# A strided slice by DMA alone: loads into 64 partitions, a new order of batches, and all stores on one queue

## The chip, the cores and the metric

One core of a Trainium2 chip. The metric is the device time of one execution in microseconds, median of several runs; the profile's span is some 1.7 us shorter. Where a run is compared with the kernel before, both ran in turn on the same chip.

## The reference

```python
def setup_inputs():
    batch, seq, dim = 32, 1024, 512
    return {"x": np.random.randn(batch, seq, dim).astype(np.float32), "start": 0, "stop": 512, "stride": 2}

def reference(x, start, stop, stride):
    return x[:, start:stop:stride, :].astype(np.float32)
```

From each of 32 batches 256 rows of 2 KB are kept, every second one of the first 512. 16.78 MB are read and 16.78 MB written. Nothing is computed.

## The kernel before

Half of the kept rows go straight from memory to memory ("direct copies", issued by ACT). The other half go into the partitions ("loads", issued by SP) and from there to the output ("stores"). Of each batch the direct copies take the kept rows of one parity, `apart(b)`, and the loads those of the other.

```python
def apart(b):
    return 1 - (b >> 1 & 1)

def two(t, b, step, parity):          # rows of one parity, of batches b and b+step
    return t[b : b + step + 1 : step].rearrange("b (p two) d -> two p b d", two=2)[parity]
...
    held = io.tile([P, B, D], x.dtype, name="held")          # P = 128
    ...
    for g in groups:                                          # 0, 8, 16, 24
        for i, (b, step) in enumerate(((0, 5), (2, 5), (1, 3), (3, 3))):
            b += g
            at = g + 2 * i
            sp.dma_start(held[:, at : at + 2], two(src, at, 1, 1 - apart(at))).then_inc(loaded[g // EIGHT], 16)
            act.dma_start(two(out, b, step, apart(b)), two(src, b, step, apart(b))).then_inc(done[1], 16)
    for g in groups:
        for queue in (sp, act):
            queue.wait_ge(loaded[g // EIGHT], 16 * 4)
        for b in range(g, g + 4):
            k = b % 2
            to = two(out, b, 4, 1 - apart(b))
            (sp, act)[k].dma_start(to, held[:, b : b + 5 : 4]).then_inc(done[k], 16)
```

Every transfer is 512 KB in packets of 2 KB, one row each.

Of the kernel before, what the change touches and what calls it, by code (L numbers as in the profile page):

```python
# [3 lines left out]

EIGHT = 8


def apart(b):


    return 1 - (b >> 1 & 1)


def two(t, b, step, parity):

    return t[b : b + step + 1 : step].rearrange("b (p two) d -> two p b d", two=2)[parity]


def kernel(tc, x, start, stop, stride, out):




    nc = tc.nc
    src = x[:, start:stop:stride, :]
    B, rows, D = out.shape
    P = rows // 2
    sp, act = nc.sync, nc.scalar
    groups = range(0, B, EIGHT)
    with tc.tile_pool(name="io", bufs=1) as io:  # L30
        held = io.tile([P, B, D], x.dtype, name="held")
        with tc.tile_critical():
            loaded = [nc.alloc_semaphore(name=f"loaded{g}") for g in groups]
            done = [nc.alloc_semaphore(name=f"done{i}") for i in range(2)]
            for g in groups:
                for i, (b, step) in enumerate(((0, 5), (2, 5), (1, 3), (3, 3))):
                    b += g
                    at = g + 2 * i
                    sp.dma_start(held[:, at : at + 2], two(src, at, 1, 1 - apart(at))).then_inc(loaded[g // EIGHT], 16)
                    act.dma_start(two(out, b, step, apart(b)), two(src, b, step, apart(b))).then_inc(done[1], 16)  # L40
            for g in groups:
                for queue in (sp, act):
                    queue.wait_ge(loaded[g // EIGHT], 16 * 4)
                for b in range(g, g + 4):
                    k = b % 2
                    to = two(out, b, 4, 1 - apart(b))
                    (sp, act)[k].dma_start(to, held[:, b : b + 5 : 4]).then_inc(done[k], 16)
            sp.wait_ge(done[0], 16 * (B // 4))
            sp.wait_ge(done[1], 16 * (B // 2 + B // 4))


# [1 line left out]
_INS = ['x', 'start', 'stop', 'stride']  # L53
_OUTS = [((32, 256, 512), 'float32')]

_NUMBERS = {'start': 0, 'stop': 512, 'stride': 2}


def kernel(**inputs):
    import numpy as _np  # L60
    import concourse.bacc as _bacc
    import concourse.tile as _tile
    from concourse import mybir as _mybir
    from concourse.bass_utils import run_bass_kernel_spmd as _run

    nc = _bacc.Bacc("TRN2", target_bir_lowering=False, num_devices=1)  # L66
    arrays, args = {}, []
    for name in _INS:
        if name in _NUMBERS:
            args.append(_NUMBERS[name])  # L70
            continue
        a = _np.ascontiguousarray(inputs[name])
        if a.dtype.kind in "iu":
            a = a.astype(_np.int64)
        arrays[f"in_{name}_dram"] = a
        args.append(nc.dram_tensor(f"in_{name}_dram", a.shape, _mybir.dt.from_np(a.dtype), kind="ExternalInput").ap())
    for i, (shape, dtype) in enumerate(_OUTS):
        dt = _mybir.dt.from_np(_np.dtype(dtype))
        args.append(nc.dram_tensor(f"out_{i}_dram", shape, dt, kind="ExternalOutput").ap())
    with _tile.TileContext(nc) as tc:  # L80
        kernel(tc, *args)
    r = _run(nc, [arrays], core_ids=[0])
    got = tuple(r.results[0][f"out_{i}_dram"] for i in range(len(_OUTS)))
    return got[0]
```

## Time and profile before

| | before |
|---|---|
| time, median (7 runs beside the first experiments) | 81.32 us |
| span of the profiled run | 79.6 us |
| first data packet | 2.0 us |
| read stage: loads and direct copies, to the last one's start | 2.0 to 54.4 us |
| store stage, to the last packet's start | 54.4 to 77.8 us |

There is no compute engine to look at. One reads the GB/s row of the page (40 equal slices of the span), the table of stretches, and the packet records, which give queue, start and duration of every 2 KB packet. The lines themselves are in the prediction below.

### The profile page before, as it was taken

What the parts mean: (1) busy time and instruction counts of PE and PEld (TensorE: products, weight loads), DVE (VectorE), ACT (ScalarE), POOL (GpSimd) and SP (SyncE); (2) the same over time, 40 slices, a digit from 0 to 9 for tenths busy, and PEclk for the clock granted to TensorE, in tenths of its full rate; (3) what the DMA queues carried; (4) which work ended last, traced back from release to release, by engine and by line L of the source; (5) the groups of instructions that cost most, each with busy time, mean ns of one, the idle gap of its engine ahead of it and who ended that gap; (6) DMA issues with size and microseconds to landing.
All of it is one profiled execution on the core that took longest, in us unless ns stands there. A gap on an engine that the chain in (4) does not pass through costs nothing. (4 is left out here: it accounts for less than half of the span.)

```text
span 79.6 us, 99 instructions
## 1 busy us (share of the span) xinstructions
POOL 0.2 (0%) x4
## 2 busy tenths in 40 slices
POOL 0000000000000000000000000000000000000000
DMA  0897999999999999999989999999999999999930
GB/s 0 258 293 231 329 282 360 364 313 322 373 300 363 367 339 369 295 327 311 259 295 398 389 361 332 297 348 407 408 408 364 351 347 348 355 357 356 350 114 5
DMA packets 13056, 25.17 MB, mean 316 GB/s; under 512 B 768, under 2 KB 768, under 8 KB 13056
## 3 DMA queue, kind: packets, MB, share of 16 engines
q1 hardware_dynamic: 6528, 12.58, 48.0%
q10 hardware_dynamic: 6528, 12.58, 47.3%
HBM read 16.78 MB, written 16.78 MB: 422 GB/s over the span
## 5 line engine op out<-in xcount | busy, mean ns | idle before, releaser
L66 POOL MEMSET const-bfloat16-1.0<- 128x1 bf16 x1 | 0.1, 101 | 0.0
L66 POOL MEMSET const-uint8-127<- 128x1 uint8 x1 | 0.1, 101 | 0.0
L66 POOL MEMSET const-float32-0.0<- 128x1 f32 x1 | 0.1, 98 | 0.2 <-issue 0.2
L66 POOL MEMSET const-float32-1.0<- 128x1 f32 x1 | 0.1, 98 | 0.0
## 6 DMA issues: line engine op xcount, KB each, us to landing
out_dram<-in_x_dram ACTq DMA_DIRECT2D x16, 512.0 KB, 22.7
held<-in_x_dram SPq DMA_DIRECT2D x16, 512.0 KB, 22.1
out_dram<-held SPq DMA_DIRECT2D x8, 512.0 KB, 21.5
out_dram<-held ACTq DMA_DIRECT2D x8, 512.0 KB, 21.4
```

The source lines that it names most:

```text
L66: nc = _bacc.Bacc("TRN2", target_bir_lowering=False, num_devices=1)
```

## The change

The stated intent: batches are loaded into 64 partitions each, in an order by which loads and direct copies read different parts of the memory, and the stores go over neighbouring batches on one queue. The diff, cut to its core:

```diff
+def pairs(t, parity):
+    return t.rearrange("(p n two) d -> two p n d", n=2, two=2)[parity]
...
+    order = [g + i for kind in ((0, 3), (1, 2)) for g in groups for i in kind]
+    sets = [order[i : i + 4] for i in range(0, len(order), 4)]
-        held = io.tile([P, B, D], x.dtype, name="held")
+        held = io.tile([P, B // 2, 2, D], x.dtype, name="held")
...
-            for g in groups:                       # loads and direct copies as above
-                ...
-            for g in groups:                       # waits by group, stores on two queues
-                ...
+            for set_of in sets:
+                for b in set_of:
+                    act.dma_start(two(out, b, 4, apart(b)), two(src, b, 4, apart(b))).then_inc(done[1], 16)
+                    for at in (b, b + 4):
+                        first = at % 2 * (P // 2)
+                        to = held[first : first + P // 2, at // 2]
+                        sp.dma_start(to, pairs(src[at], 1 - apart(at))).then_inc(loaded, 16)
+            sp.wait_ge(loaded, 16 * B)
+            for b in range(0, B, 2):
+                to = out[b : b + 2].rearrange("b r d -> (b r) d")
+                sp.dma_start(pairs(to, 1 - apart(b)), held[:, b // 2]).then_inc(done[0], 16)
```

Four things change at once: the loads' form (64 partitions, 256 KB each instead of 512), the order with the pairs of the direct copies (always b with b+4), the form of the stores, and one queue behind one wait for all loads. Below, "kind A" are the batches whose two lowest bits are 00 or 11, taken first; "kind B" those with 01 or 10.

More of the change, by code (lines that the diff above doesn't have):

```diff
@@ L29 @@
     groups = range(0, B, EIGHT)
+    order = [g + i for kind in ((0, 3), (1, 2)) for g in groups for i in kind]
+    sets = [order[i : i + 4] for i in range(0, len(order), 4)]
     with tc.tile_pool(name="io", bufs=1) as io:
-        held = io.tile([P, B, D], x.dtype, name="held")
+        held = io.tile([P, B // 2, 2, D], x.dtype, name="held")
         with tc.tile_critical():
-            loaded = [nc.alloc_semaphore(name=f"loaded{g}") for g in groups]
+            loaded = nc.alloc_semaphore(name="loaded")
             done = [nc.alloc_semaphore(name=f"done{i}") for i in range(2)]
-            for g in groups:
-                for i, (b, step) in enumerate(((0, 5), (2, 5), (1, 3), (3, 3))):
-                    b += g
-                    at = g + 2 * i
-                    sp.dma_start(held[:, at : at + 2], two(src, at, 1, 1 - apart(at))).then_inc(loaded[g // EIGHT], 16)
-                    act.dma_start(two(out, b, step, apart(b)), two(src, b, step, apart(b))).then_inc(done[1], 16)
-            for g in groups:
-                for queue in (sp, act):
-                    queue.wait_ge(loaded[g // EIGHT], 16 * 4)
-                for b in range(g, g + 4):
-                    k = b % 2
-                    to = two(out, b, 4, 1 - apart(b))
-                    (sp, act)[k].dma_start(to, held[:, b : b + 5 : 4]).then_inc(done[k], 16)
-            sp.wait_ge(done[0], 16 * (B // 4))
-            sp.wait_ge(done[1], 16 * (B // 2 + B // 4))
+            for set_of in sets:
[9 more added lines that the diff above has]
+                sp.dma_start(pairs(to, 1 - apart(b)), held[:, b // 2]).then_inc(done[0], 16)
+            sp.wait_ge(done[0], 16 * (B // 2))
+            sp.wait_ge(done[1], 16 * (B // 2))
 _INS = ['x', 'start', 'stop', 'stride']
```

## The prediction

> **What bounds the kernel now.** I read the page first, then the table of stretches, then the DMA view of single stretches. The page shows no compute at all, and the chain of waits is useless here, because it ends at the four constants that are set at the start. What remains is the DMA part.
>
> ```profile
> DMA  0897999999999999999989999999999999999930
> GB/s 0 258 293 231 329 282 360 364 313 322 373 300 363 367 339 369 295 327 311 259 295 398 389 361 332 297 348 407 408 408 364 351 347 348 355 357 356 350 114 5
> q1 hardware_dynamic: 6528, 12.58, 48.0%
> q10 hardware_dynamic: 6528, 12.58, 47.3%
> held<-in_x_dram SPq DMA_DIRECT2D x16, 512.0 KB, 22.1
> out_dram<-held SPq DMA_DIRECT2D x8, 512.0 KB, 21.5
> ```
>
> The digit row says that the 16 DMA engines are busy from end to end; the GB/s row below it says that the same 90% or more carries anything from 231 to 408 GB/s. So the engines have work all the time, and what varies is how long one packet takes. Each queue has 12.58 MB and an equal share. An issue waits some 22 us to land, so each queue has several 512 KB transfers behind the one that runs. The engines' wait list confirms it: SP waited only 0.7 us in all for loads before the stores. No semaphore is on the path today.
>
> Three stages show in the table of stretches (columns: length, POOL, clock, DMA share, GB/s):
>
> ```profile
> 2.00:14.00 12.00, 0.00 (x0) 1.00 0.93 293
> 14.00:52.00 38.00, 0.00 (x0) 1.00 1.03 335
> 52.00:60.00 8.00, 0.00 (x0) 1.00 1.04 395
> 60.00:75.00 15.00, 0.00 (x0) 1.00 1.06 353
> ```
>
> The first data packet starts at 2.0 us. Up to about 53 us the loads and the direct copies run side by side (16.78 MB: 3.51 MB in the first row, 12.75 MB in the second, the last 0.5 MB in 1.3 us of the third). From there to 77.8 us, where the last packet starts, the stores run (8.39 MB in 24.5 us, a mean of 342 GB/s with the ragged end), and 1.8 us later the span ends.
>
> The packet records say what the lost rate is made of. Of the 12,288 packets of 2 KB, most take exactly 84 ns. In the first 4,096 of each queue, 4.9% of the loads and 3.0% of the direct copies take over 200 ns, up to 1,967 ns, and many of them end within 0.1 us of one another[...]. Summed over 16 engines their excess over 84 ns is 4.2 us on the loads and 3.7 us on the direct copies; all shorter excess there is 0.7 us. From about 60 us the picture differs: no packet is over 200 ns, but over a third are between 85 and 180 ns, 2.4 us in sum. So the change has at most 8.5 us to win in the read stage and 2.4 us in the store stage. At the best rate that the trace shows (408 GB/s from 54 to 59 us) all 25.17 MB would take 61.7 us.
>
> [...] The trace agrees: equal shares, and the third row at the same 408 GB/s peak whichever mix runs. So one queue for the stores costs nothing by itself, and brings nothing by itself. [...]
>
> **The change part by part.**
>
> *Loads into 64 partitions.* 16 loads of 512 KB become 32 of 256 KB, each one batch into the lower or the upper half of the partitions. Packets stay 2 KB and bytes the same. It adds 16 transfers with their 256 completion packets (768 now, 9 ns each in the trace): 256 x 9 ns / 16 = 0.14 us. SP's issues take 434 to 1,062 ns for 512 KB while nothing backs up, so some 0.3 to 0.5 us each for half the size: 32 of them are 10 to 16 us beside 48 us of transfer, hidden. [...] the loads need only half the rate: 175 GB/s today, 205 at the peak. [...] I charge nothing in the central case and 2 to 4 us in a bad one.
>
> *The order.* First all batches with the two lowest bits 00 and 11, then those with 01 and 10, loads and direct copies of the same batches at the same time, in opposite parities of rows. Before, a load of (2, 3) ran beside a direct copy of (0, 5) or (2, 7), so the two mixed every address bit except the parity. If the stalls come from both streams meeting on one part of the memory, this takes much of the 7.9 us of long stalls away. But the first queue's loads stall even before the direct copies begin: between 2.0 and 3.5 us, with loads alone, a packet took 109 ns on average. And the direct copies' own writes stay. So I count the first stage as it is (3.51 MB, 12 us at 293, rounded to 11.7 us at 300), and give the other 13.27 MB 360 GB/s, about a third of the way from 335 to 408: 36.9 us. The read stage then ends at 2.0 + 11.7 + 36.9 = 50.6 us, against 53.3.
>
> *The seam.* Now SP waits for all 512 counts before the first store. Before, a store needed only its group of eight batches, long landed. The last load lands about 0.6 us after its packet starts, and SP's first issue needed 1.1 us to its first packet (0.94 to 2.02 us). Against these 1.7 us stands what the direct queue still has: it starts 1.5 us later, and had 161 packets (0.33 MB, 0.9 us at 360 GB/s) left when the last load packet started. That leaves 0.8 us; [...]I put 1.2 us.
>
> *The stores.* 16 transfers of 512 KB, two neighbouring batches each, on one queue. Jumps of 2 MB between packets go[...]. If that were the cause of the 353, they would run at 408: 20.6 us. I don't count on it, since the same form of store ran at 408 up to 59 us. I take 365 GB/s: 23.0 us against 24.5. Part of this is the end: today one queue runs out 1.2 us before the other, and one queue alone leaves no such tail.
>
> *Sum.* 50.6 + 1.2 + 23.0 + 1.8 (end) = 76.6 us of span. The timed median is 1.6 us over the span (81.18 against 79.6), so 78.2 us.
>
> **The rivals.**
>
> *Nothing gained, and a wait in place of none.* The stalls are of the direct copies' writes, or of anything else that the order of reads doesn't touch; the read stage stays at 53.3 us, the seam adds 1.2 and the stores save at most 0.7: 79.6 + 0.5 + 1.6 = 81.7 us. For it: loads stalled alone. Against it: the stalls come in clusters with calm stretches of 2 to 4 us between them (41 to 46 us at 381 to 414 GB/s), so they depend on what runs together.
>
> *The reads become too narrow.* Within each half the loads read one kind of address and the direct copies one other, so fewer parts of the memory share the reading[...]. Read stage 3 to 5 us longer, seam on top: 84 to 87 us. [...] Against it: 205 GB/s per stream is the most the engines give.
>
> *All as intended.* Most long stalls go (7.9 us of 8.5 come from packets over 200 ns), the stores stay at 400: 79.6 - 6 - 2.5 + 1.2 + 1.6 = 73.9 us.
>
> **Range and chances.** I weigh the intended case and its partial forms (72 to 79.5) at a little over half, since a reordering this particular was probably made from a finding about the memory that I can't see; the unchanged case at a quarter, the narrow one at a fifth. Point 78.2, range 73.0 to 84.0. Chances: faster 0.53, same 0.27, slower 0.20. The 2% line lies at 79.56 us.
>
> **What would show it.** In the profile after: the GB/s row from 14 to 50 us near 360, and few packets over 200 ns (step: order); a slice below 250 GB/s near 50 us (seam); the last 20 us at 365 or more on one queue (stores). If the load queue's packets are slower on average than the direct queue's by more than today's 3 ns, the 64 partitions cost what I didn't charge. The prediction is wrong if the read stage stays at 330 GB/s, or if stores on one queue fall below 340, or the seam is over 3 us.

## The result

The changed kernel takes 88.88 us (88.78 to 88.99, 4 runs), the kernel before 81.33 us in the same rounds: ratio 1.0923, interval 1.0857 to 1.0989. All ratios here are the mean time of one kernel's fast runs over that of the other's fast runs of the same rounds, so not quite the ratio of the medians.

The page of the changed kernel, the lines that answer to those of before (GB/s by slice of 2.2 us; the queues; the issues with their median time to landing):

```profile
GB/s 0 133 219 322 345 328 362 323 279 291 324 281 341 346 145 163 285 306 336 346 338 331 300 363 310 332 204 65 185 381 383 382 377 358 360 348 365 347 350 22
...
q1 hardware_dynamic: 8960, 16.78, 55.7%
q10 hardware_dynamic: 4352, 8.39, 36.5%
...
held<-in_x_dram SPq DMA_DIRECT2D x32, 256.0 KB, 18.5
out_dram<-held SPq DMA_DIRECT2D x16, 512.0 KB, 5.8
```

q1, with 16.78 MB, is SP's queue (loads, then stores); q10 is ACT's with the direct copies. Three holes stand out: the first two slices, two slices at 145 and 163 GB/s in the middle, and 204, 65, 185 before the stores. The table of stretches of the changed kernel (length, POOL, clock, DMA share, GB/s) is cut at these places:

```profile
2.00:5.00 3.00, 0.00 (x0) 1.00 0.72 124
5.00:31.00 26.00, 0.00 (x0) 1.00 1.00 314
31.00:35.00 4.00, 0.00 (x0) 1.00 0.91 161
35.00:56.00 21.00, 0.00 (x0) 1.00 1.01 327
56.00:60.00 4.00, 0.00 (x0) 1.00 0.79 185
60.00:62.40 2.40, 0.00 (x0) 1.00 0.16 62
62.40:71.00 8.60, 0.00 (x0) 1.00 1.02 381
71.00:85.00 14.00, 0.00 (x0) 1.00 1.05 353
```

The same view of the kernel before:

```profile
2.00:5.00 3.00, 0.00 (x0) 1.00 0.90 279
5.00:52.00 47.00, 0.00 (x0) 1.00 1.01 328
...
54.40:59.50 5.10, 0.00 (x0) 1.00 1.05 408
59.50:76.00 16.50, 0.00 (x0) 1.00 1.05 352
```

From the packet records ("behind" and "ahead" by the start of the packet with the same number in each queue):

| | before | changed |
|---|---|---|
| first packet of the loads / of the direct copies | 2.0 / 3.6 us | 5.1 / 2.4 us |
| loads relative to direct copies, after half of each | 1.9 us ahead | 6.3 us behind |
| last packet of the loads / of the direct copies starts | 52.7 / 54.4 us | 59.7 / 56.3 us |
| first store packet | 52.7 us | 62.0 us |
| last store packet | 77.8 us | 85.2 us |
| excess of packets over 200 ns, loads / direct copies | 4.2 / 3.7 us | 1.8 / 8.7 us |

A record does not say which of the 16 DMA engines took the packet. In the kernel before stores follow on the same two queues, so there the last packet of a kind and the first store are found by counting packets and are approximate: by its semaphore the last load landed at 54.4 us, in the changed kernel at 60.7 us. In the changed kernel, where the stores wait for all loads, the values are exact.

The span grew by 7.4 us. The read stage ends 5.4 us later (59.7 against 54.4), there is a gap of 2.3 us before the stores that did not exist, and the store stage, taken here from the last direct copy on, is 0.3 us shorter (23.2 against 23.5). Held against a steady 328 GB/s, the changed kernel's read stage loses about 1.9 us in the first 3 us, 1.1 us from 5 to 31 us, 2.0 us in the hole at 31 to 35 us and 1.5 us at the end, where only loads are left.

### The profile page after: what moved, and what is told of

The parts are those of the page before. It is cut to its first block, busy times and chain, and to the rows that moved or that the text cites. A ratio compares the mean times of both kernels' runs of the same rounds, so it can differ in the third digit from the quotient of the medians.

```text
span 87.0 us, 115 instructions
## 1 busy us (share of the span) xinstructions
POOL 0.2 (0%) x4
## 3 DMA queue, kind: packets, MB, share of 16 engines
q1 hardware_dynamic: 8960, 16.78, 55.7%
q10 hardware_dynamic: 4352, 8.39, 36.5%
HBM read 16.78 MB, written 16.78 MB: 386 GB/s over the span
```

## The experiments

Three theories stood against one another. **Narrow reading**: with the new order and the pairs (b, b+4) each queue reads one part of the memory at a time, which cannot serve it. **Ports** (a name alone, no record shows one): loads into 64 partitions are slower than into 128. **Seam**: one store queue behind all loads leaves a gap. A fourth, the **lag** between the two queues, came up after the first runs. A table of all timed runs first; each is explained below. "Fast" counts the fast runs of four; on a single core a run counts as slow when it is over 1.5% above the fastest of its kernel. The three measuring kernels (m_alone, m_quarters, m_rw) ran once each, so their state is unknown; only rates within one run are compared there. Chips differ between some rounds, so medians of different rounds are not to be compared closely. b_load64 and a_load128_late are slower than before, but whether by 2% is open.

| run | what it is | median us | ratio to before | fast |
|---|---|---|---|---|
| the change | | 88.88 | 1.092 | 4 |
| b_step4 | before, direct copies of b and b+4 | 87.2 | 1.069 | 3 |
| b_load64 | before, with 64-partition loads and stores of neighbours | 82.95 | 1.019 | 4 |
| b_onequeue | before, stores on one queue behind all loads | 81.82 | 1.006 | 4 |
| b_interleave | before, stores between the loads | 85.84 | 1.051 | 4 |
| a_load128 | change, 128-partition loads of 512 KB | 83.68 | 1.027 | 3 |
| a_full256 | change, 128-partition loads of 256 KB | 84.34 | 1.044 | 4 |
| a_direct256 | change, direct copies of 256 KB | 84.81 | 1.049 | 3 |
| a_late | change, loads started first | 87.2 | 1.059 | 2 |
| a_load128_late | a_load128, direct copies started first | 83.52 | 1.024 | 4 |
| a_oldorder | change, order and pairs of before | 86.17 | 1.054 | 4 |
| a_oldorder_late | a_oldorder, loads started first | 86.09 | 1.047 | 2 |
| a_setwaits | change, stores wait by parts | 88.15 | unclear | 1 |
| a_bygroup | change, kinds alternate in each group | 94.93 | 1.157 | 2 |
| a_head | change, direct copies wait for the first load | 91.56 | 1.119 | 3 |

### Each part of the change by itself, in the kernel before

**b_step4**

```diff
-((0, 5), (2, 5), (1, 3), (3, 3))
+((0, 4), (2, 4), (1, 4), (3, 4))
```

> The kernel before with one thing changed: its direct copies pair b with b+4 as in the change, instead of b with b+5 or b+3. Theory of narrow direct copies (both batches of a copy lie alike in memory, so one copy reads one part of it): 84 to 86 us, and the direct queue's packets slower than the 99 ns of before. Theory of ports (64-partition loads are the cause) and theory of the seam (one queue for the stores behind all loads): both 81 us, unchanged within 1%.

Measured 87.2 us, more than any theory said. So the pairing alone, with no other part of the change, costs 6.9%: the direct copies' mean packet goes from 99 to 106 ns, and from 5 to 31 us the rate is 288 GB/s against 328. By count the reads end at 57.5 us, but the last load landed only at 61.6 us (54.4 before), and the rate of the stores runs out slowly at the end. Why is not shown: the records don't name engines.

**b_load64**

```diff
-  sp.dma_start(held[:, at : at + 2], two(src, at, 1, 1 - apart(at)))
+  for one in (at, at + 1):
+      first = one % 2 * (P // 2)
+      sp.dma_start(held[first : first + P // 2, one // 2], pairs(src[one], 1 - apart(one)))
...
-  stores of (b, b+4)
+  stores of (b, b+1), b even, on the two queues in turn
```

> The kernel before with the loads and stores in the form of the change (one batch into 64 partitions, stores over two neighbouring batches) but the order, the direct copies, the waits by group and the two store queues as before. Theory of ports: 84 to 87 us with slower packets on the load queue. Theory of narrow direct copies and theory of the seam: 80 to 82 us.

82.95 us, 1.9% over before: between the two. The load queue's mean packet was not slower (98 against 102 ns), yet by count its loads ended 5.3 us after the direct copies (57.1 against 51.8 us), and the last one landed at 60.4 us.

**b_onequeue**

```diff
-  waits by group, stores on SP and ACT in turn
+  for g in groups: sp.wait_ge(loaded[g // EIGHT], 16 * 4)
+  all 16 stores on SP
```

> The kernel before with the stores all on one queue behind all loads, as in the change, and nothing else. Theory of the seam: 82.5 to 84 us, a gap of 1 to 2 us near 54 us in the GB/s row, and stores at 360 on average. Theory of narrow reading and theory of ports: 81 to 82 us.

81.82 us against 81.56: 0.6%, with an interval of -0.02% to 1.2%. The gap is in its records (last load packet at 53.2 us, first store packet at 54.7 us) but the direct copies, 1.2 us behind the loads, fill most of it, and the one-queue stores lose no tail. The seam alone is nearly free here.

### What one queue can do alone

**m_alone** runs six stages of 8.39 MB one after the other, each on one queue:

> A measuring kernel, right in its output: six stages of 8.39 MB each on one queue, each waiting for the one before: direct copies as before; direct copies as in the change; loads as before (128 partitions); loads as in the change (64 partitions); stores as before; stores as in the change. Theory of ports: loads of the change near 200 GB/s, loads of before 330 or more, the two forms of direct copy alike. Theory of narrow direct copies: direct copies of the change near 150 GB/s (as in the first 2 us of the changed kernel's trace), those of before 250 or more. Stores alike within 5%.

Table of stretches, each line inside one stage: direct copies of before; of the change, first kind; the moment its kinds change; its second kind; loads of before; loads of the change; stores of before; stores of the change:

```profile
10.00:27.00 17.00, 0.00 (x0) 1.00 1.01 350
35.00:53.00 18.00, 0.00 (x0) 1.00 0.81 175
55.00:59.00 4.00, 0.00 (x0) 1.00 0.93 294
62.00:76.00 14.00, 0.00 (x0) 1.00 0.89 168
85.00:105.00 20.00, 0.00 (x0) 1.00 0.97 327
120.00:134.00 14.00, 0.00 (x0) 1.00 0.91 182
165.00:180.00 15.00, 0.00 (x0) 1.00 1.05 366
190.00:205.00 15.00, 0.00 (x0) 1.00 1.05 366
```

Direct copies of the change ran at half the rate of before's, 175 and 168 GB/s against 350, except for the few us at the change of kinds (294); why not there is not shown. The two forms of the stores made no difference: 366 GB/s both, so my guess about jumps of 2 MB in before's stores was wrong. But the loads of the change are slow too (182), and this can be the 64 partitions or narrow reading.

**m_quarters** separates the two with loads alone:

> A measuring kernel, right in its output. Loads alone on one queue, 4.19 MB a stage, each stage waiting for the one before. Stages 0 to 3 use 128 partitions: batches (b, b+4) of one kind and one parity; (b, b+1), both kinds of batch, one parity rule; (b, b+3), one kind, both parities; (b, b+2), the load's rows of one kind and the direct copy's rows of the other. Stage 4: 64 partitions, neighbouring batches in turn into the lower and upper half. Stage 5: the same into the lower half only. Then two stages of direct copies in the pairs of before. Theory of narrow reading[...]: stage 0 at 165 to 185 GB/s, stages 1 and 2 at 290 or more, stage 3 at 165 to 185[...], stage 4 at 290 or more[...]. Theory of ports: stage 0 at 290 or more like the rest of the 128-partition stages, stages 4 and 5 both near 175 to 200.

```profile
4.00:26.00 22.00, 0.00 (x0) 1.00 0.94 165
31.00:41.00 10.00, 0.00 (x0) 1.00 0.99 303
49.00:61.00 12.00, 0.00 (x0) 1.00 1.00 311
66.00:87.00 21.00, 0.00 (x0) 1.00 0.95 173
93.00:107.00 14.00, 0.00 (x0) 1.00 1.06 240
114.00:130.00 16.00, 0.00 (x0) 1.00 1.07 213
```

The stages, in order: (b, b+4) 165; (b, b+1) 303; (b, b+3) 311; (b, b+2) 173; 64 partitions, halves in turn, 240; lower half alone 213. The first four use all 128 partitions, so the number of partitions has no part in them. One grouping of the rows fits their rates: **two sets, by the parity of the kept row xor the lowest bit of the batch** (set 0 where the two are equal, 1 where they differ). The sets are called areas here; where their rows lie in the memory no run shows. Beside the row's parity only the batch's three lowest bits were tried; the other two of them made no difference (165 and 173 GB/s for b+4 and b+2, 303 and 311 for b+1 and b+3). Transfers with all rows in one area ran at 165 to 173 GB/s, transfers over both areas at 303 to 311. In this grouping the loads of kind A read area 0 and its direct copies area 1; for kind B it is the other way round. So the two queues read different areas while both are in the same kind. When one is in A and the other still in B, both read one area.

The 64 partitions may count too: stages 4 and 5 reach only 240 and 213 GB/s, 13% more with the halves in turn than with the lower one alone. This test is not clean, since each of their transfers reads one area, and only successive transfers alternate between the two. But their packets look different from those of narrow reading: in stage 5 only 8% take 84 ns and 1.3% over 200 ns, in stage 0 57% take 84 ns and 29% over 200 ns.

**m_rw** looked at an oddity of the last two stages of that run: direct copies in before's pairs ran at 316 GB/s for the rows that before copies, and at 161 for the other rows, though both read both areas.

> A measuring kernel, right in its output: one queue, six stages of 8.39 MB. The pairs of direct copies of before, but taken apart: loads of the rows that before's direct copies don't read, loads of those that they do read, stores of the other rows, stores of their own, direct copies of the other rows, direct copies of their own. The measuring kernel before this one had the other rows at 161 GB/s and their own at 315, though by the rule found from the loads both read two areas. If the reading decides: stage 0 near 165 GB/s, stage 1 near 300. If the writing does: stages 0 and 1 alike at 290 or more, stage 2 near 165. If only reading and writing together: stages 0 to 3 all fast, stage 4 near 161, stage 5 near 315. If it came from the order of the stages: stage 4 fast and stage 5 slow.

Loads of either rows 323 and 322 GB/s, stores of either 365 and 366, direct copies of the other rows 159, of their own rows 319. So it is reading and writing together, and not the order of the stages. The grouping above is therefore one of reading; how reads and writes meet is not settled by these runs. It may also have a part in the 175 and 168 GB/s of the change's direct copies alone, beside the narrow reading that the loads show. Before's choice of `apart` copies directly the rows that ran at 319.

### The order

**a_bygroup** lets the kinds alternate within each group:

```diff
-    order = [g + i for kind in ((0, 3), (1, 2)) for g in groups for i in kind]
+    order = [g + i for g in groups for i in (0, 3, 1, 2)]
```

> The changed kernel with the order by groups of eight batches, both kinds in each (0, 3, 1, 2, then 8, 11, 9, 10 and so on), everything else kept. If the order itself (one kind for half of the time) is what narrows the reading: 84 to 86.5 us, since loads and direct copies then cover both kinds within a few us, and the dip at 31 to 35 us goes. If the collisions of a lagging load with a direct copy of the other kind count for more, they now come at every change of kind: 89 to 92 us.

94.93 us, beyond the second guess. Its page has the hole of the changed kernel at each early change of kind, before the queues blur:

```profile
GB/s 0 138 241 319 258 137 242 367 254 175 311 338 232 281 391 303 316 341 353 313 286 306 315 272 244 208 157 96 21 278 382 380 384 362 365 347 366 352 353 40
```

137 at about 12 us and 175 at about 21 us are below or near what one area gave alone (165 to 173). The loads are behind by 2 to 6 us here too, so at each change both queues read one area. This agrees with the reading of the hole at 31 to 35 us (161 GB/s) of the changed kernel.

**a_oldorder** undoes the order and the pairs and keeps the rest:

```diff
-            for set_of in sets:
-                for b in set_of:
-                    act.dma_start(two(out, b, 4, apart(b)), two(src, b, 4, apart(b)))
-                    for at in (b, b + 4):
+            for g in groups:
+                for i, (b, step) in enumerate(((0, 5), (2, 5), (1, 3), (3, 3))):
+                    b += g
+                    act.dma_start(two(out, b, step, apart(b)), two(src, b, step, apart(b)))
+                    for at in (g + 2 * i, g + 2 * i + 1):
```

> The changed kernel with the order of its batches and the pairs of its direct copies as before, so that each queue's transfers cover both of the memory areas found by the loads alone; 64-partition loads, one store queue and the wait for all loads kept. If the narrow reading is the main cause: 83 to 84.5 us (the 82.95 of 64-partition loads in the kernel before, and up to 1 us for the seam). If ports and seam together are the main cause: 86 us or more.

86.17 us: it takes back about 4 of the 9 per cent, and leaves 5.4%, where b_load64 and b_onequeue alone cost 1.9% and 0.6%. So narrow reading is not the main cause by itself; the loads' form and the seam cost more together than the sum of the two. The record shows how: the loads end 2.8 us after the direct copies (57.8 against 55.0), and the stores, which could have filled this time, wait for them until 59.5 us.

### The loads' form

**a_load128** gives the changed kernel back its 128-partition loads:

```diff
-                    for at in (b, b + 4):
-                        first = at % 2 * (P // 2)
-                        to = held[first : first + P // 2, at // 2]
-                        sp.dma_start(to, pairs(src[at], 1 - apart(at)))
+                    sp.dma_start(held[:, b : b + 5 : 4], two(src, b, 4, 1 - apart(b)))
...
-                sp.dma_start(pairs(to, 1 - apart(b)), held[:, b // 2])
+                sp.dma_start(two(out, b, 1, 1 - apart(b)), held[:, b : b + 2])
```

> The changed kernel with its loads back in 128 partitions (batches b and b+4 in one transfer), all else kept, stores still over neighbouring batches on one queue. Theory of ports: 84 to 86 us, and the loads that end alone run at 300 GB/s or more where the changed kernel had 202. Theory of narrow direct copies: 87.5 to 89 us, the direct queue's mean packet still about 124 ns. Theory of the seam: 88 to 89 us.

83.68 us, 2.7% over before: the largest single gain, and a little more than the theory of ports had asked for. But the loads now run within 1 us of the direct copies for most of the read stage, and the hole is gone:

```profile
2.00:5.00 3.00, 0.00 (x0) 1.00 0.77 146
5.00:31.00 26.00, 0.00 (x0) 1.00 1.01 329
31.00:35.00 4.00, 0.00 (x0) 1.00 1.02 330
```

Either the 64 partitions or the lag could have done it. This run is also the cleanest view of the order itself, with the two queues in different areas and in step. It reads at 329 GB/s, where the kernel before has 328: no gain.

**a_head** was the first try at the lag: ACT waits for the first load before it issues anything.

```diff
+            sp.dma_start(held[: P // 2, 0], pairs(src[0], 1 - apart(0))).then_inc(first_in, 16)
+            act.wait_ge(first_in, 16)
```

> The changed kernel, except that the direct queue waits for the first 256 KB load to land before it issues anything, so that the loads no longer start 2.7 us after the direct copies. Theory of the lag (the loads run 1.3 transfers behind the direct copies, so at the change of kind both queues read one area, and at the end the loads run alone): 84 to 86.5 us, the slices of 145 and 163 GB/s near 31 to 35 us weaker or gone, no loads alone at 57 to 60 us. If the 64 partitions slow the loads all the way: 88 us or more, and the loads fall behind again.

91.56 us, a miss of the design. The load had landed at 5.3 us, but the first direct packet came at 11.8 us, 6.5 us later. SP had issued six more loads meanwhile; that the direct copies waited for these is a guess. The loads now led by 5 to 11 us, and the hole grew with the lead:

```profile
GB/s 0 151 139 141 124 261 382 379 345 333 321 318 308 227 166 173 176 192 263 349 369 373 305 311 288 319 357 287 206 385 387 380 379 351 364 350 365 349 338 26
```

It lies in slices 15 to 18, some 9 us at 166 to 192 GB/s. So here a lead cost time as the lag did (161 GB/s from 31 to 35 us in the changed kernel).

**a_late, a_load128_late, a_oldorder_late** move the start by one small load of 8 KB ahead on one queue. In the changed kernel ACT's first issue took 668 ns and SP's first 64-partition load 697 ns, and ACT's transfer came first (2.4 against 5.1 us); in the kernel before SP's 128-partition load took 434 ns and came first (2.0 against 3.6 us).

```diff
+            act.dma_start(scrap[:, :], x[0, :16, :128]).then_inc(small, 16)     # on sp in a_load128_late
```

> The changed kernel with one 8 KB load ahead on the direct queue, so that its first direct copy is issued some 0.4 us later and the loads' first packet comes first. Theory of the lag: loads ahead from the start, the two slices near 150 GB/s at the change of kind become weaker than in the changed kernel, 84 to 86.5 us. Theory of ports: 88.5 to 89.5 us as before.

> The version with 128-partition loads, one 8 KB load ahead on the load queue, so that the direct copies start first as in the changed kernel. Theory of the lag: the dip at the change of kind returns and loads run alone at the end, 86 to 89 us. Theory of ports: 83.5 to 84.5 us, as without the delay.

> The changed kernel with the order and pairs of before and one 8 KB load ahead on the direct queue. With the old order a lag costs only at the end, where the loads run alone before the stores may start. Theory of the lag: 83 to 84.5 us, against 86.2 without the delay. Theory of ports: 86 to 86.5 us.

a_late: fast runs 86.08 and 86.71 us, ratio 1.059, a third of the loss back. In its profile (of a slow run) the loads led by 1.2 us at the start, but were 1.3 us behind after 0.5 MB of each and 3.5 us behind late in the stage. With 128 partitions and the direct copies first, the loads were 1.7 us behind at the start, 0.8 us soon after, and stayed at 1 us: 83.52 us, no loss. So the start matters, but the loads of the change also lose ground by themselves. a_oldorder_late has two fast runs, 85.22 and 85.55 us, against 86.17: some gain, less than expected, and its interval (1.035 to 1.059) covers the other.

**a_full256 and a_direct256** ask what makes them lose ground: partitions or size. In the change a load is 256 KB, a direct copy 512 KB.

```diff
 a_full256, against a_load128:
-  sp.dma_start(held[:, b : b + 5 : 4], two(src, b, 4, 1 - apart(b)))
+  for at in (b, b + 4):
+      sp.dma_start(held[:, at], ...the same rows of one batch...)
 a_direct256, against the change:
-  act.dma_start(two(out, b, 4, apart(b)), two(src, b, 4, apart(b)))
+  for at in (b, b + 4):
+      act.dma_start(one(out[at], apart(b)), one(src[at], apart(b)))      # one batch, 256 KB
```

> The version with 128-partition loads, but one batch of 256 KB a transfer, as in the change, instead of two. Theory of ports: 83 to 84.5 us, and the loads no more than 1.5 us away from the direct copies after the start. Theory of size[...]: the loads fall 3 us or more behind, 86 to 89 us.

> The changed kernel with its direct copies cut to one batch of 256 KB each, the size of its loads; 64-partition loads kept. Theory of size: the two queues stay within 1.5 us of each other after the start, 84 to 86.5 us. Theory of ports: the loads still fall 3 us or more behind, 88 us or more.

In these two runs size decides how the lag grows. With all 128 partitions and small loads the lag is 1.4 us after 1 MB and 3.5 us late in the stage, just as in a_late; with 64 partitions and equal sizes it stays between 0.5 and 0.7 us. The queue lines of both from 4 to 9 us (packets with the completion ones, MB, share of the engines' time), a_full256 first:

```profile
q10 hardware_dynamic: 450, 0.87, 61.3%
q1 hardware_dynamic: 315, 0.58, 34.5%
```

```profile
q1 hardware_dynamic: 442, 0.82, 48.7%
q10 hardware_dynamic: 420, 0.77, 46.8%
```

0.58 MB of loads beside 0.87 MB of direct copies in the one, 0.82 beside 0.77 in the other. So the share is 1 to 1.5 in this stretch with unequal sizes, and nearly 1 to 1 later. How the size of a transfer comes to shift the share is not shown.

In time the two runs don't separate the theories: 84.34 us for a_full256 is what the theory of ports had forecast, though the lag is what the theory of size had; 84.81 us for a_direct256 is what the theory of size had. The start explains most of it, it seems. Half way through the read stage its loads are 2.5 us behind, in a_late 2.7 and in the changed kernel 6.3. But the changed kernel's were 2.7 us behind at their first packet already, while those of the other two began 0.9 and 1.2 us ahead. All three lose 3.4 to 3.9 us from there, with 64 partitions and with 128. So somewhat under half of the changed kernel's lag is its start and the rest is size, and a_full256, with the small lag, has 289 GB/s from 31 to 35 us instead of 161.

In a_direct256 all holes of the read stage are smaller or gone (same stretches as of the changed kernel above):

```profile
2.00:5.00 3.00, 0.00 (x0) 1.00 0.72 210
...
31.00:35.00 4.00, 0.00 (x0) 1.00 1.03 346
```

210 GB/s instead of 124, and 346 instead of 161. When the sizes match, what is left to the 64 partitions, or to the smaller transfers, is the difference between a_direct256 and a_load128, 1.049 against 1.027, on different chips: some 2%. With the loads small and first in both, 64 partitions (a_late, 1.059, two fast runs) and 128 (a_full256, 1.044) have intervals that overlap.

### The seam beside the lag, and a try for more

**a_setwaits**

```diff
-            sp.wait_ge(loaded, 16 * B)
+            for i in range(3):
+                sp.wait_ge(loaded[i], 16 * 8)
+            # before the ninth store: sp.wait_ge(loaded[3], 16 * 8)
```

> The changed kernel with one semaphore for each quarter of the loads, so that the first eight stores are issued behind the loads without waiting for the last ones. Theory of the seam: 85.5 to 87 us, no gap at 59 to 62 us. If the loads' own lag is what counts and the stores only fill the lagging time: 86 to 87.5 us. No gain (88.5 us or more) would mean the seam was free.

The one fast run took 86.65 us, the other three 88.1 to 88.3 us and count as slow, so this is unclear. In the profile (of a slow run) the gap is gone, stores follow loads at 59.3 us, and the end of the store stage is ragged instead. The seam can't be worth more than 2.3 us, and this run can't say how much.

**b_interleave** issues each group's stores behind the next group's loads:

```diff
+            take(0)                       # loads and direct copies of group 0
             for g in groups:
+                if g + EIGHT < B:
+                    take(g + EIGHT)
                 ...waits and stores of g as before
```

> A try for a better kernel: the kernel before with each group's stores issued behind the loads of the next group instead of behind all loads, so that stores, loads and direct copies mix for most of the time. In the kernel before the only stretch at 395 GB/s or more was where direct copies and stores overlapped. If mixing writes from the partitions with reads takes the load off the two read areas: 74 to 79 us. If the stalls come with any reading: 80.5 to 82 us. Slower than 83 us if the waits starve a queue.

85.84 us, 5.1% slower. The stretches with stores among reads have many long packets (8% of the first 4,096 on SP's queue take over 200 ns, against 5% before). And my expectation had misread the trace: the last direct copy of the kernel before starts at 54.4 us, so the 408 GB/s from 54.4 to 59.5 us are stores alone on two queues, not a mixture. My prediction has the same misreading. No version here beat the kernel before.

## Why the prediction was wrong

*The view of the kernel before was right in the main.* The engines were busy all the time (a DMA share of 0.93 to 1.06 in every stretch from 2 to 75 us), the packets over 200 ns carried most of the loss in the read stage, and no semaphore was on the path. One line was misread: the 408 GB/s of the third stretch are not "whichever mix runs" but stores alone, so the peak that I measured the reading against is one that the reads came near only for a few us (381 to 414 from 41 to 46 us). And from 60 us on over half of the packets, not over a third, are between 85 and 180 ns; their sum of 2.4 us stands.

*The step "the order" failed.* I gave the read stage after 14 us 360 GB/s, because stalls might come from the two queues meeting. The changed kernel ran at 314 and 327 GB/s outside its holes, and with the queues in step (a_load128) it is 329, as before. The long packets moved instead of going. On the loads their excess fell from 4.2 to 1.8 us, but on the direct copies it rose from 3.7 to 8.7. In step, it is 6.7 and 1.1 us when the loads are ahead (a_load128) and 1.6 and 5.7 when they are behind (a_load128_late): sums of 7.8 and 7.3, against 7.8 in the kernel before. An estimate from m_quarters fits: two queues with an area each, at the 165 to 173 GB/s that one area gave alone, come to 330 to 346, below my 360 and with nothing in reserve. I had named this under "the reads become too narrow" and dismissed it with "205 GB/s per stream is the most the engines give", which was half of the 408 GB/s of the stores: an area gave less than that, and one queue alone more (381 GB/s for the changed kernel's stores from 62.4 to 71 us). What the order and its pairs cost by themselves, with the queues in step, is a_load128 against b_onequeue, 1.027 against 1.006: about 2%. By an estimate over half of it falls at the start, where one queue still runs alone in one area (146 GB/s from 2 to 5 us, against 270 in b_onequeue).

*The step "loads into 64 partitions" failed most.* "I charge nothing in the central case" was right about what I had looked at: from 19 to 27 us and from 37 to 49 us the loads' packets do take 84 ns on average, so there the 64 partitions cost nothing. (The rate that the loads need, 175 GB/s in my text, is 168 in the trace of before, 6.37 MB in the 38 us from 14 to 52 us.) What I did not look at is that half the size changes how the two queues share the engines (0.58 MB of loads beside 0.87 of direct copies in a_full256, 0.82 beside 0.77 with equal sizes), and that the first issue takes 0.70 us instead of 0.43 (I had estimated 0.3 to 0.5), and the direct copies start first, at 2.4 us. Both put the loads behind, by 2.7 us at the start and 3 to 6 us later. I assumed throughout that the queues keep step, since they did before (1.4 to 2.8 us apart all the way); nothing in the change keeps them in step. Removing most of the late start and the growth of the lag (a_direct256) brings 1.092 to 1.049; starting the loads first, by one small transfer (a_late), brings it to 1.059; removing lag and 64 partitions (a_load128) brings it to 1.027, which is 6.5 of the 9.2 per cent. The signal that I had named for 64 partitions, load packets slower than direct ones, did not come (94 against 124 ns), so it was the wrong sign to watch.

*The seam* I put at 1.2 us; alone it costs 0.6% (some 0.5 us). But I worked it out from a direct queue that ends after the loads. With the loads last by 3.4 us there is nothing to fill it: the loads ran alone at the end, the last one landed 1.0 us after its packet's start, and the first store's packet came 1.3 us later, so 2.3 us passed without data.

*The stores* were right: I expected 23.0 us, they took 23.2. My reason for a gain there was not: both forms ran at 366 GB/s on one queue (m_alone). In both one-queue runs the stores start faster and slow down after some 9 us: 381, then 353 GB/s in the form of the change, 377, then 358 in that of before (b_onequeue); why is not shown.

*The sum.* I had -2.7 us for the read stage, and it became +5.4 us. I had +1.2 us for the seam, and it became 2.3. Of the 10.4 us between the predicted span (76.6) and the measured one (87.0), 9.1 are the end of the read stage (59.7 against 50.6 us), 1.1 the seam and 0.2 the stores. The rival "too narrow" had named 84 to 87 us; the time lies beyond it because the order, the loads' form with its lag, and the seam cost more together than the sum of each alone: the order costs little in step, the loads' form costs little with the old order and two store queues (b_load64, 1.9%), and together with the one wait they cost 9.2%. Shown are the two rates of reading (165 to 173 GB/s in one area, 303 to 311 over both), the effect of size and of the start on the lag, and the holes. How the parts make up the 9.2% is argued: no series of runs adds them one by one on one chip. Not settled is how two queues come to share the engines, why the long packets move from one queue to the other, what makes reading and writing together slow (m_rw), and how much of the last 2% comes from the 64 partitions.

## What to carry to other kernels

A plan by which two queues read different parts of the memory held here only while they kept step (329 GB/s in step, 161 in the hole), so check their distance packet by packet, and give both transfers of the same size (a lag of 0.5 to 0.7 us with equal sizes, of 3.5 us with 256 beside 512 KB). Before stores wait for all loads, ask which queue ends last: if it is the loads, nothing hides the wait (2.3 us without data here). And when a change asks one queue to read one part of memory, measure the rate of that reading alone first; one run with a few stages would have told here.
